# Where the recurrence's outputs stand, and how its levels are spaced, in a one-core encoder block

## The chip, the cores and the metric

The kernel runs on one core of a Trainium2 chip. The metric is the device time of one execution in microseconds (us), the median over several runs. TensorE (PE) multiplies, VectorE (DVE) and ScalarE (ACT) work element by element, GpSimd (POOL) does small chores and issues some transfers, SyncE (SP) issues most of them. Each engine works through its own queue in order; semaphores tie the queues together.

## The reference, cut to what matters

One layer of an encoder for 256 tokens of width 1024: a feed-forward half, a mixer, a cross-attention on 256 memory tokens and a second feed-forward half. The mixer projects the normed input once and splits the columns: q, forget, input and output gate of a gated linear recurrence (8 heads of 128), q, k, v of a forgetting attention, and gates. The change touches the recurrence and what stands beside it:

```python
f = lb + (1.0 - lb) * jax.nn.sigmoid(f_logit)
k = 1.0 - f
...
diff = bt[:, :, :, None, :] - bt[:, :, None, :, :]
decay = jnp.exp(jnp.where(mask, diff, -jnp.inf))
a = jnp.einsum('bhtd,bhsd,bhtsd->bhts', qt, kt, decay)
o_intra = jnp.einsum('bhts,bhsv->bhtv', a, it)
...
o_a = rmsnorm(o_a, hg_norm_g[l]) * jax.nn.silu(g_a)
```

The decay between step s and step t is a product of the f between them. Everything is in float32.

## The kernel before, in words

**Products.** A projection is a sum of three products per block, since weights and activations are each split into a high part (ACT, line 136) and a low part (DVE, line 137): hi x hi, hi x lo, lo x hi. `MM` (line 92) issues every product and appends it to a list, `log`. So a place in TensorE's order has a number: the length of the list at the time.

**Placing work beside the projections.** `with after(n)` traces a block at high priority and ties each TensorE instruction in it to come behind product `log[n]`. On the other engines the block's instructions keep their data dependencies and the high priority only. A scheduler then lays out each engine's queue.

**The recurrence by levels.** In place of a scan the decayed product matrix is built by doubling: the levels 0, 1, 2, 4, 8, 16, 32, then 64 and 128. At level m, for each of the two groups of four heads (`recs`), `products` multiplies k by q for pairs of neighbouring blocks of m steps into a PSUM bank; `grow` (lines 915 to 931) multiplies the decay of a neighbouring block into q and into k on VectorE, and at level 1 zeroes parts of the result on POOL; `keep` copies the wanted entries out of PSUM, with masks on VectorE up to level 16 and with plain copies on ACT from level 32. The next level's products need the grown q and k of this one. A level up to 16 is 64 products (32 a group) of 128 x 32 by 32 or 16 columns, level 32 is 32, level 64 is 16 and level 128 is 8.

**What the levels lie in.** `r0` is the length of `log` when the recurrence begins. From there TensorE runs, in this order, the gate projection (products 0 to 143), k of the attention's first four heads (144 to 239), q of these (240 to 335), k of the second four (336 to 431) and q of these (432 to 527). Each of the four k and q steps is two rounds of 48 products, each evacuated from PSUM by VectorE (line 996). `R_AT` gives the product of this row behind which each level stands. The log-decays of the attention (`forget`) are made in the same row, behind product 174.

**What follows.** The outputs of the recurrence: for each half h of the tokens, 8 products of the matrix with the input (and for h = 1 another 8 with the first half's input) into two PSUM banks; then the sum of squares on ACT (line 257), the inverse root by eight column operations on VectorE (lines 222 to 238), and the evacuation into the gate `Gt` (line 1026). After that come three transfers by POOL of the cumulative log-decays, two selects on them (line 1036), two small transposes of `cc` whose copy is `ct` (lines 1042 and 1043), the scores of the attention (`fox_scores`, line 1047 on), and the projection v. PSUM has four `acc` banks, two `mm` banks and two `tr` banks: the levels and outputs rotate through `acc`, the projections through `mm`; the transposes for `ct` take a `tr` bank and the scores take `tr` and `acc` banks.

**Lines that the change touches:** `R_AT` (line 45), the loop over the levels (line 1002), the loop over h for the outputs (line 1015), and `ct` with its transposes (lines 1039 to 1043).

Of the kernel before, what the change touches and what calls it, by code (L numbers as in the profile page):

```python
# [16 lines left out]
P = 128  # L17
# [24 lines left out]
L_Y = 16  # L42
M_O = (24, 36)

R_AT = (18, 66, 114, 166, 226, 286, 346, 390, 430)

WARM = 8

# [29 lines left out]
def block_kernel(ctx: ExitStack, tc: tile.TileContext, wts, head_in, gf_in, x_in, mem_in, memT_in, cols, rows, fbias, masks, out):  # L78
    nc = tc.nc
    V, S, G, PE = nc.vector, nc.scalar, nc.gpsimd, nc.tensor  # L80
# [10 lines left out]
    def MM(*args, **kw):  # L91
        log.append(PE.matmul(*args, **kw).ins)  # L92

    @contextmanager
    def after(i):

        with tc.high_priority(), tc.issue_after(log[min(i, len(log) - 1)]):
            yield
# [3 lines left out]
    def nm(s):  # L102
        count[0] += 1
        return f"{s}_{count[0]}"

    def m4(shape, dt=F32, n="m"):
        return mp.tile(shape, dt, tag="m4", name=nm(n))

    def s1(n=1, dt=F32, name="s"):
        return sp.tile([P, n], dt, tag=f"s{n}", name=nm(name), bufs=16)  # L110

    def acc():
        return pp.tile([P, 512], F32, tag="acc", name=nm("acc"), bufs=4)
# [4 lines left out]
    def trp():  # L118
        return pp.tile([P, 512], F32, tag="tr", name=nm("tr"), bufs=2)
# [86 lines left out]
    ident = cp.tile([P, P], F32, name="ident")  # L206
# [52 lines left out]
    def rstd_x(src):  # L259

        s = s1(2, name="ss2")
        for j in range(2):
            ssq(s[:, j : j + 1], src[j])
        return rstd_of(s)
# [533 lines left out]
    for h in range(2):  # L798
        m = len(log)
# [152 lines left out]
    recs = [Rec(0), Rec(1)]  # L952
    r0 = len(log)
    Gt = [m4([P, D], n="G") for _ in range(2)]
    zf = [s1(8, name="zf") for _ in range(2)]
    for c in range(3):
        u = [load_split(gf_in[4 * c + i], GF) for i in range(4)]
        n = min(GF, D - c * GF)
# [10 lines left out]
    cc = sp.tile([8, T], F32, tag="fz", name="cc", bufs=1)  # L969
# [18 lines left out]
    for c in range(2):  # L988
        for name, lst, sc in (("k_b", kb_, 1.0), ("q_b", qb_, 1.0 / math.sqrt(128.0))):
            u = chunk(name, c)  # L990
            t = m4([P, 4, T], n=name)
            m = len(log)
# [7 lines left out]


    for li, m in enumerate(LEVELS + (64, 128)):
        with after(r0 + R_AT[li]):
            for r in recs:
                r.products(m)
            for r in recs:
                if m < 128:
                    r.grow(m)
            for r in recs:
                r.keep(m, li)  # L1010
    ATs, A128s = [r.AT for r in recs], [r.A128 for r in recs]


    OA = Pair()
    for h in range(2):
        ps = [acc(), acc()]
        for hd in range(8):
            g, i = hd // 4, hd % 4
            isl = slice(i * P, (i + 1) * P)
            o = ps[g][:, isl]  # L1020
            MM(o, ATs[g][:, i, h, :], iv[g][:, h, isl], start=True, stop=(h == 0))
            if h == 1:
                MM(o, A128s[g][:, i, :], iv[g][:, 0, isl], start=False, stop=True)
        r = rstd_x(ps)
        for j in range(2):
            V.scalar_tensor_tensor(out=Gt[h][:, j * 512 : (j + 1) * 512], in0=ps[j], scalar=r, in1=Gt[h][:, j * 512 : (j + 1) * 512], op0=ALU.mult, op1=ALU.mult)


    cbc = m4([P, 8, P], n="cbc")
    G.dma_start(cbc, cd[:, 0:P].partition_broadcast(P))  # L1030
    cbm = []
    for g in range(2):
# [2 lines left out]
        tv = t.rearrange("p h (b s) -> p (h b) s", b=2)  # L1035
        G.affine_select(out=tv, in_=tv, pattern=[[0, 8], [-1, P]], compare_op=ALU.is_ge, fill=BIG, base=0, channel_multiplier=1)
        cbm.append(t)

    ct = s1(16, name="ct")
    pc = trp()  # L1040
    for h in range(2):
        PE.transpose(pc[:, h * 8 : h * 8 + 8], cc[:, h * P : (h + 1) * P], ident[0:8, 0:8])
    V.tensor_copy(ct, pc[:, :16])

    ps_, pT0s, pT1s = {}, [], []

# [91 lines left out]
    m = len(log)  # L1138
# [38 lines left out]
    for c in range(2):  # L1177
        for name, X, zc in (("br_a", OA, c), ("br_b", OB, 2 + c)):
            u = chunk(name, c)
            for h in range(2):  # L1180
                z = zs[zc][:, h]
                m = len(log)
# [24 lines left out]
    m = len(log)  # L1207
# [7 lines left out]
    m = len(log)  # L1215
# [5 lines left out]
    m = len(log)  # L1221
# [77 lines left out]
    m = len(log)  # L1299
# [17 lines left out]
    m = len(log)  # L1317
# [94 lines left out]
```

## Time and profile before

| | |
|---|---|
| runs | 782.57, 782.95, 785.86 us; median 782.95 |
| the profiled execution | 783.57 us |
| its span, first to last instruction | 781.8 us |
| granted TensorE clock | 0.998 |
| data moved | 193.60 MB, mean 248 GB/s |

The stretch of the change runs from about 257 us (level 0) to about 348 us (the first product of v). In it the levels stand at 257.2, 266.2, 276.2, 284.9, 293.9, 302.6, 311.7, 318.3 and 324.3 us and the outputs at 337.7 to 343.1 us.

How to read the rows: in a timeline a row has start, length, engine, line, operation, out<-in, shape and count, and in brackets the idle time before it with what ended it. Neighbouring instructions of one kind are merged into a row. A TensorE product in full float32 shows as two records, and each record has a weight load on PEld beside it. Records overlap, since products are pipelined, so the pace is the distance from start to start. "issue" is time in which an engine waited for nothing that the profile shows. A row of a stretch has busy time and count (x) for PE, PEld, DVE, ACT and POOL, then clock, DMA share and GB/s.

### The profile page before, as it was taken

Reading aid. Unit: us, or ns where it says so; the run is one execution under the profiler, and the core shown is the slowest. Engines: PE = TensorE matmul, PEld = TensorE weight load, DVE = VectorE, ACT = ScalarE, POOL = GpSimd, SP = SyncE. Lnnn points to the kernel's source line nnn. Section 1 sums busy time; section 2 is a strip of 40 time slices with the busy share of each in tenths; the row PEclk is TensorE's granted clock in tenths of the full one; section 3 lists DMA queues with packets and bytes.
Section 4 is the critical chain, followed back from the end, with each engine's and each line's share of the span. In section 5 each row is a group of like instructions: output and inputs, shape, how many; then the busy total and the mean of one; then the engine's idle time right before and its main releaser. Section 6 shows DMA issues by size and latency. Waiting matters only on the chain.

```text
span 781.8 us, 13108 instructions
## 1 busy us (share of the span) xinstructions
PE 771.5 (99%) x4984; PEld 666.7 (85%) x4984; DVE 648.9 (83%) x999; ACT 472.9 (60%) x711; POOL 47.3 (6%) x80
## 2 busy tenths in 40 slices
PE   9999999999999999999999999999999999999996
PEld 7888878888899999988888888999888888888885
DVE  7799999999887787778778886997787987888874
ACT  7666676577753445447675434744655767777752
POOL 0000000000121100110001221012110000000000
PEclk9999999999999999999999999999999999999999
DMA  9874648377686563673489999679865199789921
GB/s 344 286 261 160 217 162 308 108 255 283 259 296 227 191 218 110 201 272 120 140 291 335 378 344 342 223 271 381 337 213 191 64 343 387 275 296 339 329 92 55
DMA packets 57390, 193.60 MB, mean 248 GB/s; under 512 B 6248, under 2 KB 9712, under 8 KB 57328
## 3 DMA queue, kind: packets, MB, share of 16 engines
q1 hardware_dynamic: 48080, 159.60, 56.7%
q0 software_dynamic: 9104, 33.04, 11.8%
q8 instruction: 39, 0.64, 0.3%
q14 instruction: 23, 0.19, 0.1%
q10 hardware_dynamic: 144, 0.13, 0.0%
HBM read 174.92 MB, written 17.83 MB: 247 GB/s over the span
## 4 chain that ended last, share of the span: by engine, by line
PE 87%; DVE 8%; issue 3%; ACT 1%; DMA 1%; DVEq 0%; ACTq 0%; SPq 0%
PE mm L92 58%; PE acc L92 24%; PE tr L92 3%; DVE lo L156 2%; DVE lo L137 2%; PE tr L324 1%; PE tr L399 1%; DMA raw<-in_wts_dram 1%; DVE sum L469 1%; DVE wide L500 1%; DVE sum L487 0%; DVE sum L465 0%; ACT hi L155 0%; ACT hi L136 0%; PE tr L1082 0%
## 5 line engine op out<-in xcount | busy, mean ns | idle before, releaser
L137 DVE TENSOR_TENSOR lo<-raw,hi 128x1024 fp32r<-128x1024 f32 (+1 forms) x220 | 261.3, 1208 | 48.0 <-ACT hi L136 44.6
L136 ACT CAST hi<-raw 128x1024 fp32r<-128x1024 f32 (+1 forms) x220 | 222.6, 1035 | 94.6 <-PE mm L92 51.1
L92 PE MATMUL mm<-lo,hT 128*128 128x512 f32 (+1 forms) x424 | 161.6, 385 | 0.0
L92 PE MATMUL mm<-hi,hT 128*128 128x512 f32 (+1 forms) x424 | 161.2, 384 | 0.0
L92 PE MATMUL mm<-hi,lT 128*128 128x512 f32 (+1 forms) x424 | 160.9, 384 | 0.0
L92 PE MATMUL acc<-hi,act 128*128 128x512 f32 x352 | 113.2, 390 | 0.0
L92 PE MATMUL mm<-hT,lo 128*128 128x256 f32 x384 | 109.4, 285 | 0.0
L92 PE MATMUL mm<-hT,hi 128*128 128x256 f32 x384 | 108.9, 284 | 0.3 <-issue 0.3
L92 PE MATMUL mm<-lT,hi 128*128 128x256 f32 x384 | 108.9, 284 | 0.0
L92 PEld LDWEIGHTS mm<-hi,hT 128*128 128x128 f32 x424 | 79.6, 188 | 15.1 <-ACT hT L285 0.5
L92 PEld LDWEIGHTS mm<-hi,lT 128*128 128x128 f32 x424 | 79.6, 188 | 14.8 <-DVE lT L286 0.5
L92 PEld LDWEIGHTS mm<-lo,hT 128*128 128x128 f32 x424 | 79.5, 188 | 14.1
L92 PEld LDWEIGHTS acc<-hi,act 128*128 128x128 f32 x352 | 66.0, 188 | 13.6
L92 PEld LDWEIGHTS mm<-hT,hi 128*128 128x128 f32 x384 | 73.6, 192 | 0.5 <-issue 0.5
L92 PEld LDWEIGHTS mm<-hT,lo 128*128 128x128 f32 x384 | 73.6, 192 | 0.2
L92 PEld LDWEIGHTS mm<-lT,hi 128*128 128x128 f32 x384 | 73.6, 192 | 0.1
L92 PE MATMUL acc<-lo,act 128*128 128x512 f32 x176 | 69.1, 393 | 0.0
L155 ACT CAST hi<-wide 128x1024 fp32r<-128x1024 f32 x44 | 45.9, 1055 | 12.8 <-DVE wide L500 7.4
L156 DVE TENSOR_TENSOR lo<-wide,hi 128x1024 fp32r<-128x1024 f32 x44 | 52.5, 1218 | 0.6 <-ACT hi L155 0.2
L794 POOL DMA_DIRECT2D sums<-wide x32 | 23.6, 737 | 347.8 <-DVE wide L791 242.8
L92 PE MATMUL mm<-hi,sh 128*128 128x512 f32 x112 | 43.9, 392 | 0.3 <-ACT keep L529 0.3
L92 PE MATMUL mm<-lo,sh 128*128 128x512 f32 x112 | 43.8, 391 | 0.2 <-DVE lo L156 0.2
(249 smaller groups left out, 1159.6 us busy)
## 6 DMA issues: line engine op xcount, KB each, us to landing
raw<-in_wts_dram SPq DMA_DIRECT2D x228, 512.0 KB, 5.4
sums<-wide POOLq DMA_DIRECT2D x32, 512.0 KB, 6.1
wide<-sums SPq DMA_DIRECT2D x32, 512.0 KB, 6.1
wide<-in_wts_dram POOLq DMA_DIRECT2D x28, 512.0 KB, 6.9
wide<-in_wts_dram SPq DMA_DIRECT2D x16, 512.0 KB, 6.4
raw<-in_gf_dram SPq DMA_DIRECT2D x12, 344.0 KB, 5.6
head<-in_head_dram SPq DMA_DIRECT2D x8, 388.0 KB, 6.0
grow<-in_rows_dram SPq DMA_DIRECT2D x4, 512.0 KB, 7.0
```

The lines of the kernel that those rows point to most:

```text
L92: log.append(PE.matmul(*args, **kw).ins)
L136: S.copy(h, r)
L137: V.tensor_tensor(out=l, in0=r, in1=h.bitcast(F32), op=ALU.subtract)
L155: S.copy(hi, src)
L156: V.tensor_tensor(out=lo, in0=src, in1=hi.bitcast(F32), op=ALU.subtract)
L324: PE.transpose(ps[:, j * P : (j + 1) * P], src(kb), ident)
L399: PE.transpose(trv[:, j, h * P : (h + 1) * P], ats[c, h][:, j * P : (j + 1) * P], ident)
L469: V.tensor_tensor(out=t4[:, i], in0=t2[:, i], in1=raws[i][:, 512:], op=ALU.add)
L500: V.tensor_tensor(out=W[:, :, 0], in0=W[:, :, 0], in1=W[:, :, 1], op=ALU.add)
L794: G.dma_start(sums[u][2 * e : 2 * e + 2, q, :, i * 512 : i * 512 + 512].rearrange("k p n -> p k n"), W[:, e])
```

## The change

Three things. Levels 4 to 128 stand closer together: 46 products apart up to level 32, then 44 and 40, where it was 52, 60, 60, 60, 44 and 40. Level 1 is issued one group at a time, the second group behind 24 further products. The outputs become a function `rec_out(h)` that is placed by `after` behind products 432 and 456, that is beside the last q projection (432 to 527), where they came behind it. `ct` and its transposes stand ahead of POOL's transfers in the program's text, where they stood behind them.

```diff
-R_AT = (18, 66, 114, 166, 226, 286, 346, 390, 430)
+R_AT = (18, 66, 114, 160, 206, 252, 298, 342, 382)
+R_OUT = 432
...
     for li, m in enumerate(LEVELS + (64, 128)):
-        with after(r0 + R_AT[li]):
-            for r in recs:
-                r.products(m)
-            for r in recs:
-                if m < 128:
-                    r.grow(m)
-            for r in recs:
-                r.keep(m, li)
+        n = r0 + R_AT[li]
+        for group in [[r] for r in recs] if m == 1 else [recs]:
+            with after(n):
+                for r in group:
+                    r.products(m)
+                for r in group:
+                    if m < 128:
+                        r.grow(m)
+                for r in group:
+                    r.keep(m, li)
+            n += 24
...
-    for h in range(2):
+    ct = s1(16, name="ct")
+
+    def rec_out(h):
         ps = [acc(), acc()]
         for hd in range(8):
...
+    with after(r0 + R_OUT):
+        rec_out(0)
+    with after(r0 + R_OUT + 24):
+        rec_out(1)
+    pc = trp()
+    for h in range(2):
+        PE.transpose(pc[:, h * 8 : h * 8 + 8], cc[:, h * P : (h + 1) * P], ident[0:8, 0:8])
+    V.tensor_copy(ct, pc[:, :16])
+
...
-    ct = s1(16, name="ct")
-    pc = trp()
-    for h in range(2):
-        PE.transpose(pc[:, h * 8 : h * 8 + 8], cc[:, h * P : (h + 1) * P], ident[0:8, 0:8])
-    V.tensor_copy(ct, pc[:, :16])
```

## The prediction, as it was put on record

> **What bounds the kernel now.** I read the busy shares first, then what TensorE waited for over the whole span, then the chain of work in order of time across the stretch that the change touches.
>
> ```profile
> PE 771.5 (99%) x4984; PEld 666.7 (85%) x4984; DVE 648.9 (83%) x999; ACT 472.9 (60%) x711; POOL 47.3 (6%) x80
> ...
> PE tr L92 <- DVE ones L205: 1.1, 1, 1.1
> PE acc L92 <- issue: 0.8, 1, 0.8
> PE tr L92 <- DVE ct L1043: 0.6, 1, 0.6
> PE mm L92 <- ACT keep L529: 0.3, 1, 0.3
> PE mm L92 <- issue: 0.3, 1, 0.3
> PE acc L92 <- DVE G L1026: 0.2, 1, 0.2
> PE mm L92 <- DVE lo L156: 0.2, 1, 0.2
> ```
>
> TensorE is busy for 99% of the span and its waits, all of them in this list, come to 3.5 us (in us: total, times, longest). The change takes no product away, so it can only win where TensorE stands still. Four of the seven waits lie in its stretch: the two called "issue" (0.8 and 0.3, where TensorE waited for no semaphore), the one for `ct` (0.6) and the one for the evacuation `G` of a recurrence output (0.2). That caps any gain far below 0.5% (3.9 us), which is about what a measurement of this kernel can tell from no change.
>
> The chain shows where the two "issue" stops lie (start, length, what):
>
> ```profile
> 267.38 0.79 issue
> 268.17 0.31 PE acc L92 x13
> 268.48 7.77 PE mm L92 x48
> ...
> 285.01 1.23 PE acc L92 x85
> 286.24 1.16 PE mm L92 x8
> 287.39 0.22 PE tr L976 x2
> 287.61 6.40 PE mm L92 x52
> ...
> 303.88 2.46 PE mm L92 x19
> 306.34 0.28 issue
> ```
>
> "PE acc" pieces are the level products (bursts), "PE mm" the projections between them. The first stop is inside level 1, the second some 20 products after level 16. What ends them is told by counts:
>
> ```profile
> q8 instruction: 39, 0.64, 0.3%
> ...
> 268.17:306.60 38.43, 38.17 (x766) 37.04 (x766) 32.36 (x60) 17.50 (x21) 2.81 (x7) 1.00 0.55 181
> ...
> L92 PEldq EVENT_SEMAPHORE  x4: 51/51/51, 273.3 to 303.1; - x4
> ```
>
> One queue moved 39 packets of instructions; TensorE's 2 x 4984 instructions over 39 is 256 a packet (0.64 MB over 39 is 16 KB). Between the two stops lie 766 matmuls, 766 weight loads and 4 semaphore instructions: 1536, exactly 6 x 256. So I read both as the wait for the next block of 256 instructions. A level up to 16 is 256 instructions in 1.2 us (128 matmul records with their loads), so a burst eats a block at once.
>
> [...]
>
> **The change part by part.** *(1) Level 1 in two groups.* From one stop, the distance to the boundaries on either side can be counted. The records around both stops:
>
> ```profile
> 266.20 1.18 PE L92 MATMUL acc<-q,k 128*32 128x16 f32 x115
> 268.17 0.31 PE L92 MATMUL acc<-q,k 128*32 128x16 f32 x13 [0.79 <-issue]
> ...
> 306.06 0.28 PE L92 MATMUL mm<-hT,lo 128*128 128x256 f32 x1
> 306.62 0.38 PE L92 MATMUL mm<-hT,hi 128*128 128x256 f32 x1 [0.28 <-issue]
> ```
>
> The boundary stands 230 instructions (115 records, 115 loads) into level 1. The one before it is 26 earlier than the burst, 13 projection products, 2.1 us at 7.77/48 = 0.16 each, so at 264.1; the block asked for there was usable at 268.17, 4.1 us later. For the second stop, 20 products and 216 instructions of a burst (1.0 us before 303.8) lie behind the boundary before it: 302.8 to 306.62, 3.8 us. Counted on from the first stop by 2 x 256, a boundary falls just inside level 4 (285.1), and the next 256 run out five products behind the piece at 287.39, at 288.0, without a stop: supply there took 2.9 us or less. With 128 instructions, 24 products and 128 more, the boundary comes 54 instructions into the second group, 6.9 us after its predecessor: covered. The stop goes. It costs more than its idle time: records of a burst start every 0.01 us and overlap by about 0.18, so 0.79 + 0.18 = **0.97 us** won. At the second stop the starts lie 0.56 apart instead of 0.12: **0.44 us**.
>
> *(2) Levels 4 to 128 closer together* (46 products instead of 52 to 60). Counting on, boundaries fall in level 2, in level 4, some 20 products behind level 4, in level 8, in level 16, in level 32: 4.9, 7.6, 3.7, 4.4, 6.5 and 6.5 us after each other. Against 2.9 to 4.1 us of supply only the 3.7 is short: 0 to 0.4. As far bound for a fetch behind data I take the median landing of a weight load:
>
> ```profile
> raw<-in_wts_dram SPq DMA_DIRECT2D x228, 512.0 KB, 5.4
> ```
>
> At 5.4 the three short distances give 0.5 + 1.7 + 1.0 = 3.2. The two measured stops are the nearer rows; I take **+0.2**, keep 0 to 3.2.
>
> VectorE must have grown q and k before the next burst. Its rows for level 4, and the longest wait of a split in front of a level:
>
> ```profile
> 285.74 0.69 DVE L920 TENSOR_TENSOR q<-q,tq 128x512 f32<-128x512 f32 x1 [0.42 <-PE acc L92]
> ...
> 287.68 0.69 DVE L921 TENSOR_TENSOR k<-k,tq 128x512 f32<-128x512 f32 x1
> ...
> 310.64 1.23 DVE L137 TENSOR_TENSOR lo<-raw,hi 128x1024 fp32r<-128x1024 f32 x1 [3.57 <-ACT hi L136]
> ```
>
> Grown 2.2 us after the burst's end (286.2 to 288.4); 46 products take 46 x 0.12 = 5.5. The slack of 3.3 us holds two weight splits of 1.23. Between the second half of level 1 and level 2 lie 24 x 0.16 = 3.8 us for one group's pair of 0.69: slack 2.4. I cost this at nothing; without the cover see rival C. The masked copies, the zero fills on POOL and the ACT copies of levels 32 to 128 move along, and the next to need them is an output 50 products (6 us) after level 128.
>
> *(3) The outputs beside the last queries.* 24 products move forward, the same in number:
>
> ```profile
> 311.39 0.28 PE L92 MATMUL mm<-hT,hi 128*128 128x256 f32 x1
> 311.51 0.28 PE L92 MATMUL mm<-lT,hi 128*128 128x256 f32 x1
> 311.72 0.38 PE L92 MATMUL acc<-q,k 128*32 128x32 f32 x11
> ...
> 312.85 0.39 PE L92 MATMUL mm<-hT,lo 128*128 128x256 f32 x1
> 313.07 0.28 PE L92 MATMUL mm<-hT,hi 128*128 128x256 f32 x1
> ```
>
> A burst of another kind inside the projections costs two edges: 0.21 and 0.22 from start to start instead of 0.12, so 0.19 an insertion. The split of level 1 adds one, the two outputs two (they stood between the projections and the next scores, which have an edge anyway): **+0.57 us**. Their follow-up work (two squares with sums on ACT, then eight column operations and two evacuations on VectorE for each half) issues no DMA. It now stands ahead of the splits of v_b on both queues, whose first use is after the scores. That goes unseen on TensorE.
>
> ```profile
> 343.38 1.16 PE L92 MATMUL tr<-k_b,q_b 128*128 128x128 f32 x8
> 345.10 0.49 PE L92 MATMUL tr<-k_b,q_b 128*128 128x128 f32 x2 [0.55 <-DVE ct L1043]
> 345.80 1.99 PE L92 MATMUL acc<-k_b,q_b 128*128 128x256 f32 x8 [0.21 <-DVE G L1026]
> ...
> 344.88 0.17 DVE L1043 COPY ct<-tr 128x16 f32<-128x16 f32 x1
> 345.00 1.41 DVE L1026 SCALAR_TENSOR_TENSOR G<-acc,rstd,G 128x512 f32<-128x512 f32 x2
> ```
>
> Today the copy `ct` and the evacuation stand behind the column operations of the outputs, and the scores need the transpose bank and the accumulators these free. Eight records at 0.11 from 343.38 would let the next start at 344.38; it started at 345.10 (0.72 lost), and the one after it at 345.80 instead of 345.32 (0.48): **1.20 us**. With the outputs done 71 products (8.5 us) before, the accumulators are free and only `ct` is made after the projections. What is late next is the last evacuation of q_b and `ct` behind a split of v_b (1.2 us) on VectorE, against some 2.9 us of scores ahead of the first that needs them. I take **+0.3** for a rest (bounds 0 and 1.2).
>
> *(4) What comes earlier with it.* POOL's loads of the decay rows wait for level 128 to free q and k:
>
> ```profile
> POOL cbc L1030 <- PE acc L92: 31.8, 1, 31.8
> ...
> 336.76 3.81 DVE L137 TENSOR_TENSOR lo<-raw,hi 128x1024 fp32r<-128x1024 f32 x2 [3.85 <-ACT hi L136]
> ```
>
> Level 128 comes 48 products and 1.4 us of stops earlier, some 7 us, and with it POOL's three transfers, its two selects and the transfers for later sums behind them. Two splits took 3.81 us today while the selects ran; that drag moves onto the outputs' column operations, which have 8.5 us. Nothing.
>
> **Sum**: -0.97 - 0.44 - 1.20 + 0.57 + 0.2 + 0.3 = -1.5 us. The profiled execution took 783.57 (span 781.8 and 1.8 around it), so 782.0; the median of the runs shown is 0.6 below it, 782.95, so **781.4**. Bounds of its own terms: all open terms at their lower ends 780.9, with `ct` unrelieved 782.3, and a few tenths of noise.
>
> **The rivals.** *A, the stops stay* (they are not bound to blocks, or come back at other places): the gain is 1.2 - 0.57 - 0.3 = 0.3, so 782.6. For it: the profile names no releaser. Against it: the 6 x 256. *B, slower: code comes late.* Bursts are denser, and if a block takes longer than 3.7 us behind data, TensorE stops behind level 4, in level 8 and in level 2. It decides over the change from a supply time of about 4.9 us (1.2 + 0.5 = 1.7 of stops eat the 1.7 won); at 5.4 it is 781.4 + 3.0 = 784.4, at 6.5 (1.6 + 2.8 + 2.1 of stops) 787.7. [...] Against it: 2.9 to 4.1 in the same traffic. *C, VectorE late*: its queue is in order, and a split that waits for ACT (3.57 above) in front of a growth takes 3.57 + 1.23 = 4.8 from a slack of 3.3; 1.5 us of stop a time, three times in six levels 4.5, so 785.9. Against it: those waits stand where VectorE had nothing else ready. That the split leaves the order as it is, because the second group's products slip behind the 24, has no separate price: it ends as A.
>
> **How the numbers follow.** The forecast 0.58, own range 780.5 to 782.7; A 0.17 (782.6); B 0.15 (784.4, tail above 787); C 0.10 (785.9, half of it beyond). The range takes in A, most of B and the runs' spread (one of the three shown lies 2.9 us over the others): 779.9 to 785.3. Faster by over 0.5% (under 779.0) would need more than the idle time that there is: 0.04. Slower by over 0.5% (above 786.9) is the tail of B and C: 0.10. Within: 0.86.
>
> **What would show it.** Among TensorE's waits of the changed kernel, "issue" at level 1 and the waits for `ct` and `G` are gone or under 0.3 in all; level 1 shows two bursts of 64 records; the chain has no "issue" piece between level 2 and level 32. An "issue" piece 256 instructions apart behind level 4 or in level 8 is B; a wait of a burst for `k` or `q` on VectorE is C. A wait in the v_b projections for `lo` or `v_b`, or any change after the scores, would say that I overlooked what follows.

## The result, and the profile after

The changed kernel took 781.80 us, median of 16 runs (780.58 to 782.53), beside 783.69 for the kernel before in 16 runs on the same chip (781.86 to 785.86). The ratio is 0.9978, with a 95% interval of 0.9971 to 0.9986: 1.7 us less (1.1 to 2.3), within the 0.5% that had been called no change. The forecast was 781.4.

First the busy shares of the changed kernel, then all that its TensorE waited for over the whole span (total, times, longest):

```profile
PE 770.6 (99%) x4984; PEld 667.4 (86%) x4984; DVE 649.7 (83%) x999; ACT 473.3 (61%) x711; POOL 49.2 (6%) x80
```

```profile
PE tr L93 <- DVE ones L206: 1.1, 1, 1.1
PE mm L93 <- issue: 0.4, 1, 0.4
PE mm L93 <- ACT keep L530: 0.2, 1, 0.2
```

The lines of the changed kernel are one higher up to the levels. As many products as before are busy for 0.9 us less, and seven waits have become three. Both old "issue" stops, the wait for `ct` and the one for `G` are gone; one "issue" of 0.4 is new. The chain of the changed kernel (the work that ended last, in order of time) says where (start, length, what):

```profile
258.00 7.78 PE mm L93 x48
265.78 0.67 PE acc L93 x51
266.44 3.98 PE mm L93 x24
270.42 0.67 PE acc L93 x51
271.09 3.99 PE mm L93 x24
275.08 1.25 PE acc L93 x100
...
284.35 1.87 PE mm L93 x14
286.22 0.22 PE tr L977 x2
286.44 0.47 PE mm L93 x4
286.91 0.37 issue
287.29 3.60 PE mm L93 x28
```

Level 1 stands there as two bursts of 64 records (the piece counts 51, since overlapped records are left to their neighbours), with 24 products between and no stop. Behind level 4 there are 14 products, two transposes, 4 products, and then the new stop. Two rows of the chain of the kernel before give the other end of the comparison:

```profile
266.27 1.11 PE acc L92 x77
...
276.25 1.25 PE acc L92 x100
```

From the start of level 1 to that of level 2 it was 9.98 us (276.25 - 266.27), and is 9.30 (275.08 - 265.78): 0.68 won.

For the stretch's other end serve the transposes for `ct` and, further on, those of the output gate `G`, the first TensorE work behind the scores and v that is the same in both. Timeline of TensorE, kernel before:

```profile
343.17 0.28 PE L1042 MATMUL tr<-ident,cc 8*128 8x8 f32 x2
...
363.01 1.03 PE L324 MATMUL tr<-ident,G 128*128 128x128 f32 x8
```

Changed kernel:

```profile
286.63 0.28 PE L93 MATMUL mm<-lT,hi 128*128 128x256 f32 x1
287.29 0.39 PE L93 MATMUL mm<-hT,lo 128*128 128x256 f32 x1 [0.37 <-issue]
...
341.90 0.28 PE L1040 MATMUL tr<-ident,cc 8*128 8x8 f32 x2
...
360.43 1.03 PE L325 MATMUL tr<-ident,G 128*128 128x128 f32 x8
```

From the start of level 0 (257.19 before, 256.68 after) to those transposes of `G` is what I call **the stretch** from here on: 363.01 - 257.19 = 105.82 us before, 360.43 - 256.68 = 103.75 after, so 2.07 won. Behind it the two profiles differ by less than 0.1; ahead of it they differ by 0.51 us already, which is none of the change and moves from run to run. The experiments are therefore compared by their stretch, in one profiled execution each, and by the ratio of their time to that of the kernel before.

Within it: 19.84 us from the `ct` transposes to the `G` transposes before, 18.53 after, so 1.31 won there. The same 146 records of the last q projection and the outputs, in their old and new order (a stretch's length; busy time and count of PE, PEld, DVE, ACT, POOL; clock, DMA share, GB/s), first before, then after:

```profile
326.20:343.17 16.97, 16.97 (x146) 16.85 (x145) 9.72 (x13) 6.99 (x13) 4.68 (x7) 1.00 0.81 275
```

```profile
324.95:341.90 16.95, 16.95 (x146) 16.82 (x144) 13.01 (x29) 6.67 (x13) 5.13 (x4) 1.00 0.62 221
```

TensorE needs the same time for them either way. VectorE has 3.3 us more to do inside it and nobody on TensorE waits for it.

### The profile page after: what moved, and what is told of

Its sections match the earlier page's. It is cut to its first block, busy times and chain, and to the rows that moved or that the text cites. A ratio compares the mean times of both kernels' runs of the same rounds, so it can differ in the third digit from the quotient of the medians.

```text
span 779.3 us, 13113 instructions
## 1 busy us (share of the span) xinstructions
PE 770.6 (99%) x4984; PEld 667.4 (86%) x4984; DVE 649.7 (83%) x999; ACT 473.3 (61%) x711; POOL 49.2 (6%) x80
## 4 chain that ended last, share of the span: by engine, by line
PE 90%; DVE 6%; DMA 2%; ACT 1%; issue 1%; DVEq 0%; SPq 0%; ACTq 0%
PE mm L93 59%; PE acc L93 24%; PE tr L93 3%; DVE lo L157 1%; DVE lo L138 1%; PE tr L325 1%; DMA wide<-in_wts_dram 1%; PE tr L400 1%; DMA raw<-in_wts_dram 1%; DVE sum L470 1%; DVE wide L501 1%; DVE sum L466 0%; ACT hi L156 0%; PE tr L1091 0%; DVE act L157 0%
```

## The experiments

### One part of the change alone

**Kernel before with the new loop over the levels only** (old `R_AT`, old place of the outputs).

```diff
+        n = r0 + R_AT[li]
+        for group in [[r] for r in recs] if m == 1 else [recs]:
+            with after(n):
...
+            n += 24
```

> The kernel before with level 1 in two groups 24 products apart, nothing else. Measured on TensorE's stretch from the first record of level 0 to the first transpose of G: 105.8 us before the change, 103.75 after it. Theory (blocks of 256 instructions that need about 4 us to come): the stop in level 1 (0.97 with its tail) goes, an insertion (0.2 to 0.3) is added, the stop behind level 16 and the waits for ct and G stay where they were, because the count of instructions ahead of them is the same: stretch 105.1, time 0.7 us under before. Rival A (stops belong to the place, not to a count): one half of level 1 still has an issue stop, stretch 106.0, time the same or 0.2 over.

Measured: 782.88 us, ratio 1.0 (0.999 to 1.0009); stretch 104.84, 0.98 less. The stop in level 1 is gone and the waits for `ct` (0.5) and `G` (0.2) stay, as expected. Against the expectation the stop behind level 16 is gone too, although the count of instructions up to it is the same, and one of 0.23 stands behind level 4, at a count where the kernel before had none in its list. So a stop at an unchanged count (0.28 in the kernel before, none here) can come and go from one execution to another. The time does not confirm the microsecond of the trace: its interval allows 0.8 us at most.

**Kernel before with the outputs and `ct` moved only.**

```diff
+    with after(r0 + R_OUT):
+        rec_out(0)
+    with after(r0 + R_OUT + 24):
+        rec_out(1)
```

> The kernel before with the outputs behind products 432 and 456 and ct moved ahead of the transfers; levels spaced as before, level 1 whole. Theory: both issue stops stay (0.79 and 0.28), the waits for ct and G (1.2 from start to start) go; stretch 104.5, time 1.3 us under before, whether or not level 128, now only 25 products ahead of the second output, has been copied in time (its copy took 1.08 us, 24 products last 2.9). Rival (the outputs need the closer levels): the second output waits for the copy of level 128 and gives back 0.5 us or more.

Measured: 782.09, ratio 0.9986 (0.9976 to 0.9996); stretch 104.12, 1.70 less. The waits for `ct` and `G` are gone, the stop in level 1 stays (0.68), and the move itself costs nothing. POOL's selects stand as late as before (335.87), so the outputs and `ct` earlier are enough to end those waits. The stop behind level 16 is gone here too although the count up to there is unchanged, and one of 0.18 stands behind level 4.

**Kernel before with the new spacing only.**

```diff
-R_AT = (18, 66, 114, 166, 226, 286, 346, 390, 430)
+R_AT = (18, 66, 114, 160, 206, 252, 298, 342, 382)
```

> The kernel before with the new places of levels 4 to 128, level 1 whole, outputs behind the last queries. Theory: the stop in level 1 stays (0.97), the one behind level 16 goes (0.44), one some 20 products behind level 4 comes (0.53 in the changed kernel), the waits for ct and G stay since the outputs stay: stretch 105.8 to 105.9, time within 0.3 us of before. Rival (the spacing itself wins, by taking VectorE's work forward): stretch under 105.3.

Measured: 781.59 (780.66 to 784.6), ratio 0.9984 (0.997 to 0.9998). The profiled execution was the longest of them: its two stops, at the same counts as ever, had 1.56 us (level 1) and 1.26 (behind level 4), so its stretch was 106.08. The median is 1.3 us under the kernel before by the ratio, where no difference over 0.3 had been expected. What neither theory had: **the waits for `ct` and `G` were gone although the outputs stood behind the queries as before.** The timeline of this kernel shows why:

```profile
329.04 3.87 POOL L1036 TENSOR_SCALAR_AFFINE_SELECT cbm<-cbm 128x1024 f32<-128x1024 f32 x2 [4.79 <-DMA cbm<-cd]
...
339.04 2.36 DVE L137 TENSOR_TENSOR lo<-raw,hi 128x1024 fp32r<-128x1024 f32 x2 [3.80 <-ACT hi L136]
...
345.49 0.28 PE L1042 MATMUL tr<-ident,cc 8*128 8x8 f32 x2
...
345.81 0.17 DVE L1043 COPY ct<-tr 128x16 f32<-128x16 f32 x1
```

Level 128 stands 48 products earlier, so POOL's two selects run at 329 and not at 336, and the two weight splits that VectorE makes just ahead of `ct` take 2.36 us and not the 3.81 they took beside the selects. `ct` follows its transposes by 0.32 us (345.81 - 345.49); in the kernel before it was 1.71 (344.88 - 343.17). So in these rows two splits took longer beside the selects; why is not shown. A theory that this is a sufficient cause by itself was put to the next run.

**Kernel before with levels 64 and 128 earlier only**, all else as it was.

```diff
-R_AT = (18, 66, 114, 166, 226, 286, 346, 390, 430)
+R_AT = (18, 66, 114, 166, 226, 286, 346, 372, 400)
```

> The kernel before with level 64 behind product 372 instead of 390 and level 128 behind 400 instead of 430, nothing else; outputs behind the last queries. It frees q and k, and with them POOL's transfers and two selects, 3.6 us earlier. Theory (the waits for ct and G came from VectorE being held up while POOL's selects ran: two splits took 3.81 us instead of 2.4): the selects now end before the last splits, VectorE's chain of the first output ends 1.2 to 1.5 us earlier, the waits for ct and G go with the outputs where they were; issue stops as before (0.4 to 1.0 in all); stretch 105.8 - 1.2 = 104.6, time 1.2 us under before. Rival (ct was late because the outputs stood late): the waits stay, stretch 105.8.

Measured: 782.64, ratio 0.9991 (0.9982 to 1.0); stretch 105.08. Against the expected 104.6 it has 0.45 us of a stop behind level 4, one of three at the old counts: 0.57 in level 1, 0.45 behind level 4, 0.53 behind level 16. The waits for `ct` and `G` are gone, and its timeline agrees:

```profile
328.94 3.52 POOL L1036 TENSOR_SCALAR_AFFINE_SELECT cbm<-cbm 128x1024 f32<-128x1024 f32 x2 [4.77 <-DMA cbm<-cd]
...
336.85 2.36 DVE L137 TENSOR_TENSOR lo<-raw,hi 128x1024 fp32r<-128x1024 f32 x2 [3.85 <-ACT hi L136]
```

So this gain has two sufficient causes in the change, and either alone brings it: the outputs and `ct` earlier, or levels 64 and 128 earlier. By the time alone the second is only just told from none (its interval ends at 1.0).

### The stops: bound to the count of instructions?

**Kernel before with 16 small products more at the start of the program** (64 instructions), which shifts every later boundary and nothing else.

```diff
+    for _ in range(16):
+        MM(wps[0:32, 0:16], ones[:, 0:32], ones[:, 0:16], start=True, stop=True, tile_position=(0, 0))
```

> The kernel before with 16 small products (64 instructions on TensorE, their result not used) ahead of everything; no place, spacing or output is changed. Theory (the stop in level 1 follows the count of instructions): the boundary that stood 230 instructions into level 1 now stands 167 into it, and the one before it 44 products ahead of the burst, so the block is there in time: no stop in level 1, none 20 products behind level 16. Stops of up to 0.7 us can come at new places, 221 instructions into level 4 and 232 into level 16, where a boundary stands just ahead of the burst; the waits for ct and G (1.2) stay, since nothing moves POOL's selects: stretch 104.4 to 105.8. Rival A (the stop belongs to level 1): it stays at 0.5 or more at record 115 of level 1.

Measured: 782.3, ratio 0.9991 (0.9977 to 1.0004); stretch 104.58. The chain runs through level 1 without a stop, 9.00 us from its start to that of level 2; the only stop of the recurrence, 0.03 us, is inside level 4, where the count puts the boundary:

```profile
266.81 1.23 PE acc L92 x84
268.04 7.77 PE mm L92 x48
275.81 1.25 PE acc L92 x102
...
284.58 1.08 PE acc L92 x76
285.66 0.03 issue
```

and `ct` stays late beside late selects, in the list of waits and in the timeline:

```profile
PE tr L92 <- DVE ct L1045: 0.8, 1, 0.8
```

```profile
335.68 1.09 POOL L1038 TENSOR_SCALAR_AFFINE_SELECT cbm<-cbm 128x1024 f32<-128x1024 f32 x1 [8.89 <-DMA cbm<-cd]
...
335.86 4.01 DVE L137 TENSOR_TENSOR lo<-raw,hi 128x1024 fp32r<-128x1024 f32 x2 [3.85 <-ACT hi L136]
```

Sixteen products far ahead of the recurrence took both stops out of it (1.24 us less of stretch) and left the wait for `ct`. The stop in level 1 belongs to the count; the wait for `ct` does not. For the stop behind level 16 this run alone shows little, since that one was also gone at an unchanged count. By the time, the gain is not told from none.

**The changed kernel with the same 16 products.** Same edit.

> The changed kernel with 16 small products (64 instructions on TensorE, their result not used) ahead of everything, in the time in which TensorE waits for its first data; nothing else moves. Theory (stops come every 256 instructions, wherever that falls): the boundaries lie 64 instructions earlier in the work, so stops of about 2.3 us right behind level 0, 1.4 in level 4 and 0.4 behind level 16 stand in place of the one of 0.37 behind level 4; stretch 103.75 + 3.6 = 107.3, time 3 to 4 us over the changed kernel. Rival A (place or density): the stretch stays at 103.75 and the time within 0.3 us of the changed kernel.

Measured: 781.29, ratio 0.9972 (0.9962 to 0.9982); stretch 103.13, and no "issue" at all. The expectation of 3 to 4 us of stops fell. That the stop behind level 4 went with the count was right; that a boundary just inside level 0 and one right behind it must stop TensorE was wrong. Between 250 and 257.3 us one packet of the queue that moves TensorE's instructions lies ahead of level 0 (which starts at 257.37 in this kernel), and none there in the changed kernel. It landed at 256.20, 1.17 us ahead of level 0, so in this execution a block was there before TensorE came to its boundary. When a block is asked for was not shown.

**The changed kernel with 64 small products behind level 4**, first all at one tile position.

```diff
+    extra = trp()
+    with after(r0 + 90):
+        for _ in range(64):
+            MM(extra[0:32, 0:16], ones[:, 0:32], ones[:, 0:16], start=True, stop=True, tile_position=(0, 0))
```

> The changed kernel with 64 small products (256 instructions, their result not used) more, which stand some 17 projection products behind level 4, where the changed kernel has its issue stop. The suspected cost doubled: boundaries fall just inside the added products and again just behind them, 256 instructions that run in 1.2 us. Theory (a block needs about 4 us from the time the one before it is entered): a stop of 2.5 to 3.5 us behind the added products beside their own 1.2 and edges of 0.2; stretch 103.75 + 4.5 = 108.2, time about 4 us over the changed kernel. Rival (no supply limit): own cost alone, stretch 105.2, time 1.4 us over the changed kernel.

Measured: 785.86, ratio 1.0036 (1.0022 to 1.005); stretch 108.24. Inconclusive: the added products ran at 33 ns a record and not at the 10 ns of a level, so their own time covers the block. Timeline:

```profile
287.95 4.10 PE L93 MATMUL tr<-ones 128*32 128x16 f32 x124 [0.38 <-issue]
```

Then with the four tile positions of a level in turn:

```diff
+        for i in range(16):
+            for k in range(4):
+                MM(extra[32 * k : 32 * k + 32, i * 16 : i * 16 + 16], ones[:, 32 * k : 32 * k + 32], ones[:, i : i + 16], start=True, stop=True, tile_position=(0, 32 * k))
```

> As the run with the doubled burst, but the 64 added products go to four places of the array in turn, as the level products do, so that they run at the levels' pace (128 records in 1.2 us, where those at one place took 33 ns a record and were no dense block). They fall some 17 projection products behind level 4; a boundary stands a few instructions into them and the next one just behind their end. Theory (a block needs about 4 us from the entry into the one before it): a stop of 2 to 3.5 us right behind the added products; stretch 103.75 + 1.4 + 2.7 = 107.9. Rival (no supply limit; the stops seen are something else): own cost alone, stretch 105.2, no stop over 0.5.

Measured: 786.89, ratio 1.0049 (1.003 to 1.0069); stretch 108.83. Timeline of TensorE behind the added products:

```profile
288.06 1.46 PE L93 MATMUL tr<-ones 128*32 128x16 f32 x126
...
292.29 0.58 PE L93 MATMUL mm<-hT,lo 128*128 128x256 f32 x1 [2.10 <-issue]
```

Dense now (126 records in 1.4 us), and TensorE stands for 2.10 us in the middle of plain projections, which wait for no other engine, at the record where 256 instructions since the boundary before are used up. Counted back by 128 records, that boundary was crossed at 288.29, so the next block was usable 4.0 us later; in the changed kernel, counted the same way (21 records behind level 4 and the last 107 of its own), it is 283.22 to 287.29, 4.07 us. Both lie between the 3.8 and 4.1 that the prediction had read off. The rest of the extra time was no part of either theory, see the last section.

**What ends a stop.** The traces also hold the time of each packet on that queue (q8), and these say more than the counts. The two kernels with 256 instructions more move 40 packets on it, all others 39. In the stretch all fourteen profiles together have 16 stops of TensorE with "issue"; every one stands at the same remainder of the count of TensorE's instructions by 256, and every one ends 1.2 to 1.6 us after a packet has landed. So I read a stop as the wait for a block, and its length as that by which the packet is late. From the entry into the block before to the end of the stop it was 3.2 to 5.0 us. For the stop in level 1, at the same count in five profiles (us):

| kernel | packet begins after the entry of the block before | packet takes | landing to the end of the stop | stop |
|---|---|---|---|---|
| before | 1.53 | 1.37 | 1.21 | 0.79 |
| outputs moved | 1.57 | 0.96 | 1.46 | 0.68 |
| spacing only | 2.49 | 0.97 | 1.42 | 1.56 |
| levels 64 and 128 earlier | 1.16 | 1.34 | 1.40 | 0.57 |
| changed, level 1 whole | 1.58 | 0.96 | 1.31 | 0.52 |

The same reading explains the stop behind level 16. With the old spacing and the old count the packet there took 1.97 us in the kernel before (stop 0.28); with level 1 split and with the outputs moved it took 1.13 and 1.25, and there was no stop; with levels 64 and 128 earlier it took 1.01 but began 1.87 us after the entry (stop 0.53). Why a packet begins or ends late in one execution and not in another is not shown.

### Is the split of level 1 needed?

**The changed kernel with level 1 whole again**, behind product 66.

```diff
-        for group in [[r] for r in recs] if m == 1 else [recs]:
-            with after(n):
...
+        with after(r0 + R_AT[li]):
+            for r in recs:
+                r.products(m)
```

> The changed kernel with level 1 whole again, the rest of the change kept. Stretch from level 0 to the first transpose of G 103.75 us in the changed kernel. Theory (code supply): the stop in level 1 is back (0.8 to 1.6, as in the two runs that had it whole), one insertion (0.28) less, the stop behind level 4 (0.4 to 1.3) stays, no wait for ct or G: stretch 104.3 to 105.2, time 0.5 to 1.4 us over the changed kernel. Rival (the split has no part in the gain): no stop in level 1, stretch 103.5.

Measured: 781.79 (780.55 to 785.42), ratio 0.9991 (0.9976 to 1.0007); stretch 103.64. The stop is back at the old place in level 1, with 0.52 us; and the one behind level 4, at an unchanged distance from its boundary, did not show. The expectation (a stretch of 104.3 to 105.2, and 0.5 to 1.4 us over the changed kernel) did not come true: by the stretch the split was worth nothing in these two executions (103.75 with it), and the medians are equal (781.79 and 781.80, taken on two chips). It exchanges one stop for another.

**Level 1 whole, but at places of the row where no block is short:**

```diff
-R_AT = (18, 66, 114, 160, 206, 252, 298, 342, 382)
+R_AT = (18, 78, 114, 150, 206, 252, 298, 342, 382)
```

> The changed kernel with level 1 whole and the places (18, 78, 114, 150, 206, ...): level 1 twelve products later and level 4 ten earlier, so that by count no block of 256 instructions holds nearly a whole burst: a boundary falls 207 instructions into level 1 with the one before it 24 products ahead of the burst, then about 135 into level 2, 62 into level 4, 200 into level 8, 110 into level 16. Theory: no issue stop, one insertion less than in the changed kernel; stretch 103.75 - 0.28 - 0.5 = 103.0, time 0.7 us under the changed kernel. Rival (a burst of 256 instructions stops TensorE wherever the boundary lies): a stop of 0.5 or more in level 1; rival C (VectorE late): a burst waits for q or k.

Measured: 780.99 (780.39 to 782.11), ratio 0.9976 (0.9966 to 0.9985); stretch 102.82, no "issue". The changed kernel and this one were then run once more, side by side on one chip.

> The changed kernel again, beside the next one on the same chip: 1.2 to 2.2 us under before, runs within 2 us of each other, a stop of 0.2 to 0.6 behind level 4.

> The version with level 1 whole behind product 78 and level 4 behind 150, timed beside the changed kernel. Theory: 0.5 to 0.8 us under the changed kernel (no issue stop, one insertion less). Rival (run-to-run spread covers it): the same within 0.3 us.

Measured: the changed kernel 781.58 (780.58 to 783.16), ratio 0.9979 (0.9966 to 0.9992), stretch 103.54 with a stop of 0.15 behind level 4; the respaced one 780.93 (780.11 to 782.21), ratio 0.9971 (0.9959 to 0.9983), stretch 102.81. Its chain runs through the levels without a stop; levels 1 and 2:

```profile
268.01 1.23 PE acc L93 x85
269.23 5.88 PE mm L93 x36
275.11 1.25 PE acc L93 x102
```

It is the shortest version of all, and its interval lies wholly below the kernel before. Against the changed kernel it is 0.7 and 0.9 us shorter in the traces and 0.65 by the medians, but the intervals of the two ratios overlap, so the time alone does not separate them.

## Why the prediction was right

The forecast came true: 781.80 for 781.4, and 1.7 us less for 1.5. Three of its mechanisms are the ones that the runs show: the stop in level 1, the new stop behind level 4, and the wait for `ct` and `G`. That the sum agrees so closely is partly luck, for the terms are off in both directions, and one of them (the stop behind level 16) came true in part by chance. The kernel before, 782.95 in the three runs known then, has 783.69 in sixteen, so the difference tells more than the absolute 781.4. Fourteen products fewer between two levels take 1.68 us less, read between levels 8 and 16, where neither profile stops (8.62 and 6.94); with that, in us, over the stretch:

| term | forecast | the traces |
|---|---|---|
| level 1: stop gone, one insertion more | -0.97 + 0.19 | -0.68 |
| level 4 to level 8, beside 14 products less | +0.2 | +0.44 |
| level 16 to level 32, beside 14 products less (stop behind level 16) | -0.44 | -0.52 |
| the outputs' two insertions | +0.38 | 0 |
| `ct` and `G` | -1.20 + 0.3 | -1.31 |
| sum | -1.54 | -2.07 |

**Step 1, level 1: right.** The stop was bound to the count and was a wait for a block, shown by the shift of 64 instructions, by the split alone, and by the packets. The kernel with the shift has level 1 whole and without a stop: 9.00 us to level 2. Against it the stop cost 0.98 (9.98 - 9.00; forecast 0.97) and the insertion 0.30 (9.30 - 9.00; forecast 0.19). The stop itself has no fixed size. At the same count of instructions it had 0.52 to 1.56 us in five profiles. One profile of it was enough to say where, but not how much.

**The stop behind level 16: right number, partly by chance.** The changed kernel has none, as forecast, but with the old spacing two of four profiles have none either. The prediction took a stop seen once for one that comes every time. So the 0.52 of this pair of profiles is not shown to be the work of the respacing.

**Step 2, the new stop: right in place, undersized.** It was put some 20 products behind level 4 and stands behind 18 products and two transposes. The bounds 0 to 0.4 were formed with a block that had come in 2.9 us or less; in the dense place it takes 4.07. Start to start it is 0.66 (287.29 - 286.63) instead of 0.12, and the product behind it loses another 0.1 to an edge: 0.63 in all, as the kernel with level 1 whole shows, which has no stop there (7.13 us from level 4 to level 8 in the chain, 284.02 to 291.15, against 7.76 here). The table has less, 0.44, because the kernel before lost 0.2 at the same boundary, too little at a time for its list of waits. Its timeline:

```profile
287.81 0.28 PE L92 MATMUL mm<-lT,hi 128*128 128x256 f32 x1
288.00 0.39 PE L92 MATMUL mm<-hT,lo 128*128 128x256 f32 x1
288.23 0.28 PE L92 MATMUL mm<-hT,hi 128*128 128x256 f32 x1
```

The starts lie 0.19 and 0.23 apart instead of 0.12, and the packet had landed at 286.64, 1.36 us before 288.00. So the block came in 2.9 us and not in less. In other executions of the same place the stop was 1.26, 0.15 and none. The prediction's own sign, no "issue" piece between level 2 and level 32, did not come true: this piece is the sign of rival B, at a small price. The cover on VectorE held: no burst waits for q or k.

**Step 3, the outputs: the term of the insertions was mis-sized.** The price of 0.19 was read from the level bursts and carried over to the outputs. Those are products of 128 columns in full float32, 16 records for 8 products. They go in like this (timeline of the changed kernel):

```profile
324.95 0.28 PE L93 MATMUL mm<-hT,hi 128*128 128x256 f32 x1
325.07 1.95 PE L93 MATMUL acc<-iv,f 128*128 128x128 f32 x16
326.77 0.36 PE L93 MATMUL mm<-lT,hi 128*128 128x256 f32 x1
```

There is no gap ahead, and the 1.70 us from 325.07 to 326.77 is 16 records at 0.106; in the two stretches above the same records take no longer with both insertions (16.95 against 16.97). The row that I took for the price was the nearest one by what it interrupted, not by its shape.

**Step 3, `ct`: right that the wait goes, and for the reason given.** The prediction said that the accumulators are free once the outputs stand earlier, and that some 2.9 us of scores then lie ahead of the first product that needs `ct`. TensorE and VectorE of the changed kernel:

```profile
343.11 1.89 PE L93 MATMUL acc<-k_b,q_b 128*128 128x256 f32 x8
344.84 1.05 PE L93 MATMUL tr<-k_b,q_b 128*128 128x128 f32 x8
```

```profile
328.27 1.91 DVE L138 TENSOR_TENSOR lo<-raw,hi 128x1024 fp32r<-128x1024 f32 x1
...
340.81 2.36 DVE L138 TENSOR_TENSOR lo<-raw,hi 128x1024 fp32r<-128x1024 f32 x2 [2.66 <-ACT hi L137]
...
343.76 0.17 DVE L1041 COPY ct<-tr 128x16 f32<-128x16 f32 x1
```

`ct` itself comes no earlier: it starts 1.86 us after its transposes (343.76 - 341.90), where it was 1.71. But TensorE now has eight products of the scores to do first, and the transposes that need the bank of `ct` start 2.94 us after those for `ct` (344.84 - 341.90). So nothing waits, and the rest of 0.3 did not come. The kernel with only the outputs and `ct` moved has the same 18.53 us from the transposes for `ct` to those of `G` (361.40 - 342.87).

The second sufficient cause was overlooked. Step (4) cost the earlier selects of POOL at "nothing". It had seen that two splits took 3.81 us beside the selects, but not that these two stand in VectorE's queue ahead of `ct`, so that freeing them brings `ct` forward by itself: the kernels with earlier levels show that, with `ct` 0.3 us behind its transposes and again 18.5 us up to those of `G`. In the changed kernel the drag lies on a split further up, 1.91 us for 1.2, and costs nothing. Since either cause alone gives all of it, neither can be given a share.

**The rivals.** A (stops stay) is refuted for level 1; for level 16 it is not settled. B (code late) is real as a mechanism: the added dense products made 2.10 us of it behind level 4. Its price did not come because the supply behind level 4 took 4.1 and 3.9 us in the changed kernel's two profiles, under the 4.9 from which it decides. That is no fixed limit: in the longest execution of the kernel with the new spacing alone it was 4.9 and 5.0 us, which made its stops of 1.56 and 1.26. All these times are counted from the entry into the block before; that the next block is asked for there was the prediction's assumption. The 5.4 of rival B was the landing of a weight load; no run shows code waiting behind such a load, and the longest supply took 5.0 (the 39 packets of code took 0.88 to 1.97 us each in the kernel before and 0.88 to 1.84 in the changed one). C did not occur: in no profile does a burst of a level wait for q or k.

What stays open: when a block of code is asked for, why its packet begins up to 1.3 us later in one execution than in another, and whether the spread of the kernel before (to 786.6 us, against 783.2 for the changed one) comes from it. A stop of 1.56 us in an execution of 784.6 speaks for it; the kernel shifted by 64 instructions, whose profile has no stop in level 1 and which also had a run of 784.34, speaks against. No run was made for it.

## What to carry to other kernels

A stop without a releaser in a TensorE that is otherwise full is worth counting instructions for, to see whether two such stops lie a multiple of 256 apart, as here. What took them away in these runs was 16 small products further up (1.24 us less of stretch), or bursts respaced so that by count no 256 instructions pass in less than about 4 us (no stop in either of two executions, though the slowest supply here took 5.0); the new spacing of the change also brought one elsewhere (0.37 behind level 4). A stop seen in one profile can be absent from the next of the same kernel, so look at several before its length enters a sum. Before a wait is put down to the work ahead of it in its queue, look at how long that work takes when nothing runs beside it; the neighbour that slows it can be moved instead. Look also at what TensorE could do first: a copy that stays late costs nothing if other products stand ahead of the one that needs it. The price of an insertion is taken from a row of the same shape of product, or both prices are kept as bounds.

## What was not expected of the hardware

**After a stop of 2.1 us TensorE ran at half speed.** In the kernel with 64 dense products added, the stretches behind the stop show the granted clock (the third value from the end):

```profile
290.00:292.29 2.29, 0.19 (x3) 0.00 (x1) 0.00 (x0) 1.64 (x2) 0.00 (x0) 0.95 0.04 14
292.29:294.30 2.01, 2.01 (x9) 2.01 (x10) 0.00 (x0) 0.00 (x0) 0.00 (x0) 0.50 0.03 8
294.30:296.30 2.00, 2.00 (x15) 2.00 (x14) 0.83 (x3) 0.00 (x0) 0.00 (x0) 0.71 0.00 0
296.30:298.30 2.00, 2.00 (x133) 1.87 (x134) 1.21 (x3) 0.00 (x0) 0.54 (x1) 1.00 0.00 0
```

At 0.50 the products start 0.21 apart and not 0.12, for some 3 us. That is why this experiment cost 5.08 us of stretch, with 1.4 of added products, 2.1 of stop, and the rest from some 16 products that were 0.09 slower each. Stops of 1.26 and 1.56 us, in the kernel with the spacing alone, were followed by products 0.12 and (in the gate projection) 0.16 apart as ever. So the half clock was seen once, behind the stop of 2.10 us (2.38 from start to start); what brought it about is not shown.

**The small products ran at 33 ns a record at one tile position, and at 11 at four positions in turn** (4.10 us for 124 records, 1.39 for 126).
